# Seven-product stages of a two-block network: the way back's factors loaded through one queue into the large pool

## The chip, the cores and the metric

The kernel runs on one core of a Trainium2 chip. Its time is the device time of one execution in microseconds (us). A profile of one execution shows what each engine did: TensorE (PE, with its weight loads as PEld), VectorE (DVE), ScalarE (ACT), GpSimd (POOL) and SyncE (SP), which here only issues transfers. A transfer (DMA) is issued by an instruction in the queue of SP or ACT; if it has to wait for data or for a free buffer, that queue stands until then. TensorE's clock is throttled; the share that was granted is listed beside each stretch.

## The reference

Two network blocks over one sequence of 1024 tokens of width 1024, in float32. What matters here are the three places with a wide hidden layer:

```
h = h + square(relu(z @ w_up)) @ w_down                     # block 1: 1024 -> 4096 -> 1024
x = x + 0.5 * norm(swiglu(h, ffn1_w_in, ffn1_w_out))        # block 2: 1024 -> 2816 -> 1024
x = x + 0.5 * norm(swiglu(h, ffn2_w_in, ffn2_w_out))        # block 2: the same again
```

Between the first and the second lies a gated projection, between the second and the third a mixer with attention and a state-space model (`s5_mixer`: 32 groups of 64 complex states), whose tables depend on parameters alone.

## The kernel before

Each matrix is cut into a high and a low part (`hi` rounded on ACT, `lo` = value minus `hi` on DVE or POOL), and a product is the sum of three matmuls (hi x hi, hi x lo, lo x hi). The three wide layers use a scheme with seven products of half-size blocks instead of eight. The way up (`ups_s`, L526) writes sums of blocks of the hidden layer, the LEFT factors, to memory (`lay_by`, L607: tiles `hs`, on SP's queue). The way back, which the change touches, is `down_s` (L644). It is called three times: stage 1 for `w_down` (16 pairs of row blocks, 8 quads `q` of two), stages 2 and 3 for `ffn1_w_out` and `ffn2_w_out` (11 pairs, 6 quads, the last of one).

A stage runs its products in the order 2, 1, 5, 3, 6, 7, 4. Products 2 and 1 write four banks each, 1 in `a`; 5 and 3 accumulate in `c`; 6, 7 and 4 in `a` again. There are eight banks. When a product ends, its `out` empties banks into `Y`: a copy on ACT (L743, after products 2, 5, 3 and 4) or an addition on DVE (L744, after 1, 6, 7).

A product is a row of units, one for each quad. A unit (L702) loads a left factor `sd` from `hs` (SP, L706, into the tag `raw`, which has two buffers), obtains a right factor, cuts both into hi and lo (`pair`, L698 and L699), and gives PE 24 matmuls (L717). The right factor comes in one of two ways:

- Stage 1 (`wt`, L655, and `right`, L671): blocks of the weight `wd` are loaded on ACT's queue (L659) into the large pool `u` (32 slots of 512 KB over all partitions) and kept in `W`, so that products 5, 6, 7 and 4 form their differences in place on DVE (L673). Block 2 alone is loaded twice.
- Stages 2 and 3 (`kept`, L663): the differences were made during the way up (`rights`, L625) and lie in memory as `tw`; one load `td` for each unit, on ACT's queue (L667).

`after(ins, first)` (L299) orders the schedule alone: the program is laid out by a simulated run, in which `ins` is placed no earlier than the end of `first`; no semaphore on the chip stands for it. On the chip, each engine and queue runs its instructions in the order of the schedule and waits for data and for free slots. Loads of right factors are placed after the end of the product before the last (`ends`), or of the last product 3 of the way up (`self.late`). Left loads are placed in one chain with all other loads into `raw` (`last_raw`).

The state-space tables are made during stages 1 and 2, so that they take no time of their own: `s5_small` (L1234) and eight parts `s5_eighth` (L1337), each with a first step (a load of `xy`, which has one buffer; multiplications on DVE and POOL) and a second step (transposes L1388 and small matmuls on PE into two banks, copies on ACT, eight small transfers L1412 on SP). `aside` says ahead of which product which steps are called. A call sets the place in the program's order, which is the priority in the schedule.

Of the kernel before, what the change touches and what calls it, by code (L numbers as in the profile page):

```python
# [11 lines left out]
F32 = mybir.dt.float32  # L12
# [6 lines left out]
P = 128  # L19
# [3 lines left out]
H = 512  # L23
# [224 lines left out]
class Model:  # L248
# [395 lines left out]
    def down_s(self, hs, w, Y, done, z=None, aside={}, tail=1, tw=None):  # L644

        nc = self.nc
        v = nc.vector
        npair = w.shape[1]  # L650
        qs = [(p, min(2, npair - p)) for p in range(0, npair, 2)]
        W = {}
        ends = [self.late]

        def wt(b, q):  # L655
            if (b, q) not in W:
                p, n = qs[q]
                t = W[b, q] = self.u("wd", shape=[P, 2, H])
                d = nc.scalar.dma_start(out=t[:, :n], in_=w[b, p : p + n].rearrange("c p f -> p c f"))  # L659
                self.after(d, ends[max(len(ends) - 2, 0)])  # L660
            return W[b, q]

        def kept(p, q):  # L663
            n = qs[q][1]
            t = self.u("td", shape=[P, 2, H])
            src = tw[q][self.RIGHT[p], :n] if p in self.RIGHT else w[{2: 2, 1: 0, 3: 3}[p], 2 * q : 2 * q + n]
            d = nc.scalar.dma_start(out=t[:, :n], in_=src.rearrange("c p f -> p c f"))  # L667
            self.after(d, ends[max(len(ends) - 2, 0)])
            return t

        def right(p, q):  # L671
            n = qs[q][1]
            sub = lambda o, x, y: v.tensor_tensor(o[:, :n], x[:, :n], y[:, :n], op=ALU.subtract)  # L673
            if p == 2:
                t = wt(2, q)
                del W[2, q]
            elif p == 1:
                t = wt(0, q)
            elif p == 5:
                t = wt(0, q)  # L680
                sub(t, wt(1, q), t)
            elif p == 3:
                t = wt(3, q)
            elif p == 6:
                t = wt(0, q)
                sub(t, wt(3, q), t)
            elif p == 7:
                t = wt(1, q)
                sub(t, wt(3, q), t)
            else:  # L690
                t = wt(2, q)
                sub(t, t, wt(0, q))
            return t

        def pair(tags, x, n):
            hi, lo = (self.u("tt", F32R, [P, 2, H]) if tag == "u" else self.pw.tile([P, 2, H], F32R, name=tag, tag=tag)
                      for tag in tags)
            nc.scalar.activation(hi[:, :n], x[:, :n], AF.Copy)  # L698
            v.tensor_tensor(lo[:, :n], x[:, :n], hi.bitcast(F32)[:, :n], op=ALU.subtract)  # L699
            return hi, lo  # L700

        def unit(p, q):  # L702
            n = qs[q][1]
            g, i = self.LEFT[p]
            s = self.pr.tile([P, 2, H], F32, name="sd", tag="raw")
            d = nc.sync.dma_start(out=s[:, :n], in_=hs[q][g][i, :n].rearrange("c p f -> p c f"))  # L706
            self.after(d, self.last_raw)
            self.last_raw = d
            if tw:
                return pair(("wh", "wl"), s, n), pair(("u", "u"), kept(p, q), n)  # L710
            return pair(("wh", "wh"), s, n), pair(("wl", "wl"), right(p, q), n)

        def mm(bank, un, c, t, start, stop):
            (sh, sl), (th, tl) = un
            ts = slice(t * P, (t + 1) * P)
            for k, (x, y) in enumerate(((sh, th), (sh, tl), (sl, th))):
                self.mark = nc.tensor.matmul(bank, x[:, c, ts], y[:, c], start=start and k == 0, stop=stop and k == 2,  # L717
                                             skip_group_check=True)

        def product(p, banks, start, out, mid=None):  # L720
            nq = len(qs)
            head = nq - (tail if p == 4 else 1)
            for q in range(head):
                un = unit(p, q)
                for c in range(qs[q][1]):
                    for t in range(4):
                        mm(banks[t], un, c, t, start and q == 0 and c == 0, False)
                if q % 2 and chores:
                    chores.pop(0)()
            uns = [(q, unit(p, q)) for q in range(head, nq)]  # L730
            if mid:
                mid()
            for t in range(4):
                for q, un in uns:
                    for c in range(qs[q][1]):
                        mm(banks[t], un, c, t, start and q == 0 and c == 0, q == nq - 1 and c == qs[q][1] - 1)
                out(t)
            ends.append(self.mark)

        chores = []  # L740
        four = lambda: [self.bank() for _ in range(4)]
        A, B = slice(0, H), slice(H, D)
        copy = lambda t, sl, b: nc.scalar.activation(Y[t][:, sl], b, AF.Copy)  # L743
        plus = lambda t, sl, b: v.tensor_tensor(Y[t][:, sl], b, Y[t][:, sl], op=ALU.add)  # L744

        def also(p):
            for f in aside.get(p, ()):
                f()

        def c11(t):  # L750
            Y[t] = self.u("Y")
            copy(t, A, b[t])

        def c22(t):
            Y[4 + t] = self.u("Y")
            copy(4 + t, B, c[t])

        def c12(t):
            plus(t, B, a[t])
            chores.append(lambda: done(t))  # L760

        def c21(t):
            copy(4 + t, A, a[t])
            done(4 + t)

        also(2)
        b = four()
        product(2, b, True, c11)
        also(1)
        a = four()  # L770
        product(1, a, True, lambda t: plus(t, A, a[t]))
        also(5)
        c = four()
        product(5, c, True, c22)
        also(3)
        product(3, c, False, lambda t: copy(t, B, c[t]))
        also(6)
        product(6, a, False, c12)
        also(7)
        if z:  # L780
            chores.append(lambda: z.flush(3))
        product(7, a, False, lambda t: plus(4 + t, B, a[t]))
        also(4)
# [941 lines left out]
```

## Time and profile before

| | us |
|---|---|
| median of three runs | 3072.33 (3070.43 to 3072.9) |
| profiled execution | 3082.47 |
| its span, first to last instruction | 3080.7 |
| PE busy | 2821.6 (92%) |
| DVE, ACT, POOL busy | 1775.9, 1323.5, 868.0 |

Mean granted clock 0.963. Stage 1 lies between 603.7 and 978.0 us of the span, stage 2 between 1571.1 and 1828.8, stage 3 between 2828.4 and 3068.0. In each, the first number of a row is where it starts; "idle before <-releaser" is how long the engine had nothing to run, and which instruction or transfer ended that. A row of busy time by stretch gives its bounds and length, the busy time and the count of instructions of PE, PEld, DVE, ACT and POOL (of those asked for, where it is for one line or one tile), the granted clock, the busy share of the DMA engines and the GB/s that they moved; a row of sums gives the stretches of one stage together.

### The profile page before, as it was taken

To read this page: it belongs to the slowest core of one execution; us is meant where nothing else is said; L and a number is where in the kernel's file an instruction comes from. 1 tells how busy PE (TensorE), PEld (TensorE's weight loads), DVE (VectorE), ACT (ScalarE), POOL (GpSimd) and SP (SyncE) were. 2 spreads that over 40 slices of the span, in tenths; PEclk is the share of its full clock that TensorE was granted. 3 is DMA by queue.
4 is the path that set the end of the run, shared out by engine and by line. 5 is a ranking of instruction groups with operands and counts; after the bars stand their busy time and mean duration, and the time that the engine had idled before them with its cause. 6 is when DMAs were issued, how large, how long until landed. Compare 5 with 4: busy or idle time off the path is not lost.

```text
span 3080.7 us, 33834 instructions
## 1 busy us (share of the span) xinstructions
PE 2821.6 (92%) x12585; PEld 2306.2 (75%) x12585; DVE 1775.9 (58%) x2527; ACT 1323.5 (43%) x1921; POOL 868.0 (28%) x667
## 2 busy tenths in 40 slices
PE   8998999898999979999978999997689899998998
PEld 7777788677777858777767778886677677776776
DVE  4576655487784365665667551417635756665445
ACT  5446555433445463333324452246644533333343
POOL 3331332211222432121111031459844212211002
PEclk9999999999999989999989999998899999999999
DMA  3114344564455123454466661523113244446556
GB/s 141 61 42 137 132 146 146 201 230 144 162 183 170 55 82 103 151 177 150 146 221 212 217 220 72 168 76 110 35 48 130 86 150 158 158 157 208 181 180 209
DMA packets 192309, 443.11 MB, mean 144 GB/s; under 512 B 23220, under 2 KB 23312, under 8 KB 192144
## 3 DMA queue, kind: packets, MB, share of 16 engines
q1 hardware_dynamic: 155600, 362.83, 35.4%
q10 hardware_dynamic: 36544, 78.13, 7.2%
q8 instruction: 98, 1.61, 0.2%
q14 instruction: 67, 0.55, 0.1%
HBM read 303.92 MB, written 131.60 MB: 141 GB/s over the span
## 4 chain that ended last, share of the span: by engine, by line
PE 62%; DMA 14%; DVE 9%; ACT 6%; issue 6%; POOL 2%; SPq 1%; ACTq 0%; DVEq 0%; POOLq 0%
PE b L541 22%; PE b L717 17%; PE b L455 4%; PE b L442 4%; DMA raw<-in_f_out 3%; DMA raw<-in_f_in 3%; DMA td<-tw 2%; DMA tw<-raw 2%; PE b L1103 2%; PE b L1101 2%; PE b L1102 2%; DMA sd<-hs 1%; ACT wh L481 1%; PE b L1624 1%; DVE wl L482 1%
## 5 line engine op out<-in xcount | busy, mean ns | idle before, releaser
L541 PE MATMUL b<-zh,wh 128*128 128x512 f32 x1680 | 644.9, 397 | 30.5 <-ACT wh L481 23.1
L541 PE MATMUL b<-zh,wl 128*128 128x512 f32 x1680 | 623.3, 392 | 8.4 <-DVE wl L482 3.3
L541 PE MATMUL b<-zl,wh 128*128 128x512 f32 x1560 | 612.8, 393 | 15.4 <-DVE zl L211 15.4
L717 PE MATMUL b<-tt,wh 128*128 128x512 f32 x1232 | 392.1, 400 | 51.8 <-ACT tt L698 46.5
L541 PEld LDWEIGHTS b<-zh,wh 128*128 128x128 f32 x1680 | 319.5, 190 | 117.2 <-ACT wh L481 35.1
L541 PEld LDWEIGHTS b<-zh,wl 128*128 128x128 f32 x1680 | 316.8, 189 | 78.6 <-DVE wl L482 4.6
L717 PE MATMUL b<-wl,wh 128*128 128x512 f32 x1344 | 323.5, 402 | 40.3 <-ACT wl L698 26.3
L541 PEld LDWEIGHTS b<-zl,wh 128*128 128x128 f32 x1560 | 295.4, 189 | 79.5 <-DVE zl L211 19.2
L717 PEld LDWEIGHTS b<-wl,wh 128*128 128x128 f32 x1344 | 258.7, 194 | 102.4 <-ACT wl L698 27.8
L717 PEld LDWEIGHTS b<-tt,wh 128*128 128x128 f32 x1232 | 237.5, 194 | 106.8 <-ACT tt L698 48.9
L482 POOL TENSOR_TENSOR wl<-raw,wh 128x1024 fp32r<-128x1024 f32 x60 | 148.0, 2469 | 392.4 <-ACT wh L481 368.9
L698 ACT ACTIVATE wh<-sd 128x1024 fp32r<-128x1024 f32 x140 | 141.7, 1014 | 254.3 <-PE b L717 127.0
L717 PE MATMUL b<-tt,wl 128*128 128x512 f32 x616 | 244.1, 397 | 0.0
L352 POOL TENSOR_TENSOR wl<-raw,wh 128x1024 fp32r<-128x1024 f32 (+1 forms) x58 | 142.6, 2464 | 305.0 <-ACT wh L351 274.1
L481 ACT ACTIVATE wh<-raw 128x1024 fp32r<-128x1024 f32 x120 | 126.8, 1059 | 226.0 <-DMA raw<-in_f_in 102.6
L383 POOL TENSOR_SCALAR v<-ss 128x1 f32<-128x1 f32 x80 | 46.4, 580 | 497.6 <-ACT junk L376 493.9
L618 POOL TENSOR_TENSOR hw<-h 128x512 f32<-128x512 f32 x38 | 59.2, 1558 | 409.2 <-DVE h L1188 173.2
L699 DVE TENSOR_TENSOR tt<-td,tt 128x1024 fp32r<-128x1024 f32 x84 | 95.2, 1134 | 115.4 <-ACT tt L698 115.2
L698 ACT ACTIVATE tt<-td 128x1024 fp32r<-128x1024 f32 x84 | 83.0, 988 | 162.7 <-DMA td<-tw 86.2
L699 DVE TENSOR_TENSOR wl<-sd,wh 128x1024 fp32r<-128x1024 f32 x84 | 97.4, 1159 | 77.1 <-ACT wh L698 77.1
L505 DVE TENSOR_TENSOR s<-raw 128x512 f32<-128x512 f32 x60 | 75.2, 1253 | 115.2 <-DMA raw<-in_f_in 105.2
L717 PEld LDWEIGHTS b<-tt,wl 128*128 128x128 f32 x616 | 119.1, 193 | 25.3
(362 smaller groups left out, 5301.0 us busy)
## 6 DMA issues: line engine op xcount, KB each, us to landing
sd<-hs SPq DMA_DIRECT2D x126, 512.0 KB, 4.0
raw<-in_f_in SPq DMA_DIRECT2D x94, 512.0 KB, 3.5
raw<-in_f_out SPq DMA_DIRECT2D x44, 512.0 KB, 3.6
tw<-raw SPq DMA_DIRECT2D x44, 512.0 KB, 2.9
wd<-in_w_down ACTq DMA_DIRECT2D x40, 512.0 KB, 8.9
td<-tw ACTq DMA_DIRECT2D x40, 512.0 KB, 4.3
hs<-h SPq DMA_DIRECT2D x38, 512.0 KB, 3.3
hs<-hw SPq DMA_DIRECT2D x38, 512.0 KB, 3.1
```

The lines of the kernel that those rows point to most:

```text
L352: nc.gpsimd.tensor_tensor(l, r, h.bitcast(F32), op=ALU.subtract)
L442: nc.tensor.matmul(pp[n], w[:, k, :], z(m, k, slice(n * H, n * H + H)), start=k == 0 and w is wh and m == 0, stop=k == nk - 1 and w is wl)
L455: yield nc.tensor.matmul(pp, h[:, ts], w[:, sl], start=f == 0 and w is wh and h is hh, stop=f == len(hs) - 1 and h is hl)
L481: nc.scalar.activation(hi.rearrange("p a b -> p (a b)"), x, AF.Copy)
L482: eng.tensor_tensor(lo.rearrange("p a b -> p (a b)"), x, hi.bitcast(F32).rearrange("p a b -> p (a b)"), op=ALU.subtract)
L505: v.tensor_tensor(s1, a21, a22, op=ALU.add)
L541: self.mark = nc.tensor.matmul(bank, w, x, start=start and k == 0 and i == 0, stop=k == 3 and i == 2, skip_group_check=True)
L698: nc.scalar.activation(hi[:, :n], x[:, :n], AF.Copy)
L699: v.tensor_tensor(lo[:, :n], x[:, :n], hi.bitcast(F32)[:, :n], op=ALU.subtract)
L717: self.mark = nc.tensor.matmul(bank, x[:, c, ts], y[:, c], start=start and k == 0, stop=stop and k == 2, skip_group_check=True)
L1101: nc.tensor.matmul(pp, zh, wh[:, k % 2, :], start=k == 0, stop=False)
L1102: nc.tensor.matmul(pp, zh, wl[:, k % 2, :], start=False, stop=False)
```

## The change

All loads of the way back go through one function, `load`: on SP's queue, into the pool `u`, placed after the end of the unit that lies three (stage 1) or four (stages 2 and 3) units back; `ends` now takes one entry for each unit. The left factors leave the tag `raw` and its chain. Of the weight's blocks in stage 1 only block 0 is kept (`W[q]`); the others are loaded where they are needed, so that product 7 loads two and product 5, 6 and 4 one each. The rounded right factors of stage 1 move from the tag `wl` to the pool `u`, as in the other stages. The steps in `aside` are called after the second unit of a product instead of ahead of it.

```diff
+        ahead = 4 if tw else 3
+
+        def load(name, src, q):
             n = qs[q][1]
-            t = self.u("td", shape=[P, 2, H])
-            src = tw[q][self.RIGHT[p], :n] if p in self.RIGHT else w[{2: 2, 1: 0, 3: 3}[p], 2 * q : 2 * q + n]
-            d = nc.scalar.dma_start(out=t[:, :n], in_=src.rearrange("c p f -> p c f"))
-            self.after(d, ends[max(len(ends) - 2, 0)])
+            t = self.u(name, shape=[P, 2, H])
+            d = nc.sync.dma_start(out=t[:, :n], in_=src.rearrange("c p f -> p c f"))
+            self.after(d, ends[max(len(ends) - ahead, 0)])
             return t
 
         def right(p, q):
-            n = qs[q][1]
+            k, n = qs[q]
+            if tw and p in self.RIGHT:
+                return load("td", tw[q][self.RIGHT[p], :n], q)
+            block = lambda b: load("wd", w[b, k : k + n], q)
             sub = lambda o, x, y: v.tensor_tensor(o[:, :n], x[:, :n], y[:, :n], op=ALU.subtract)
...
+            t = block({2: 2, 1: 0, 5: 1, 3: 3, 6: 3, 7: 3, 4: 2}[p])
+            if tw or p in (2, 3):
+                return t
+            if p == 1:
+                W[q] = t
+            elif p in (5, 6):
+                sub(W[q], t, W[q])
+                return W[q]
             elif p == 7:
-                t = wt(1, q)
-                sub(t, wt(3, q), t)
+                sub(t, t, block(1))
             else:
-                t = wt(2, q)
-                sub(t, t, wt(0, q))
+                sub(t, t, W.pop(q))
             return t
...
-            s = self.pr.tile([P, 2, H], F32, name="sd", tag="raw")
-            d = nc.sync.dma_start(out=s[:, :n], in_=hs[q][g][i, :n].rearrange("c p f -> p c f"))
-            self.after(d, self.last_raw)
-            self.last_raw = d
-            if tw:
-                return pair(("wh", "wl"), s, n), pair(("u", "u"), kept(p, q), n)
-            return pair(("wh", "wh"), s, n), pair(("wl", "wl"), right(p, q), n)
+            s = load("sd", hs[q][g][i, :n], q)
+            return pair(("wh", "wl"), s, n), pair(("u", "u"), right(p, q), n)
...
                         mm(banks[t], un, c, t, start and q == 0 and c == 0, False)
+                ends.append(self.mark)
+                if q == 1:
+                    for f in aside.get(p, ()):
+                        f()
                 if q % 2 and chores:
```

The functions `wt` and `kept`, and the seven calls `also(p)` ahead of the products, are gone.

## Rows read from the trace of the kernel before

**Rows 1.** Busy time by stretch: sums over stages 1, 2, 3; two single stretches.

```profile
819.80:978.00 158.20, 147.09 (x690) 118.86 (x689) 115.54 (x197) 69.25 (x84) 40.19 (x60) 0.97 0.53 181
...
sum 374.30, PE 333.74 PEld 269.48 DVE 273.27 ACT 150.66 POOL 73.09; mean PE 47.68 PEld 38.50 DVE 39.04 ACT 21.52 POOL 10.44
...
sum 257.70, PE 227.29 PEld 185.32 DVE 151.99 ACT 112.14 POOL 43.36; mean PE 32.47 PEld 26.47 DVE 21.71 ACT 16.02 POOL 6.19
...
2977.60:3007.50 29.90, 29.90 (x134) 24.76 (x133) 14.96 (x15) 13.65 (x16) 0.00 (x0) 1.00 0.63 211
...
sum 239.60, PE 218.09 PEld 178.46 DVE 117.59 ACT 95.69 POOL 14.52; mean PE 31.16 PEld 25.49 DVE 16.80 ACT 13.67 POOL 2.07
```

**Rows 2.** PE's instructions in order of time, at the twelve longest waits.

```profile
615.15 1.22 PE L717 MATMUL b<-wl,wh 128*128 128x512 f32 x2 [11.38 <-ACT wl L698]
...
669.06 1.22 PE L717 MATMUL b<-wl,wh 128*128 128x512 f32 x2 [6.01 <-ACT wl L698]
...
769.39 1.22 PE L717 MATMUL b<-wl,wh 128*128 128x512 f32 x2 [4.86 <-ACT wl L698]
...
949.36 1.32 PE L717 MATMUL b<-wl,wh 128*128 128x512 f32 x4 [4.04 <-ACT wl L698]
...
953.05 1.22 PE L717 MATMUL b<-wl,wh 128*128 128x512 f32 x2 [2.37 <-DVE wl L699]
...
1587.56 2.95 PE L717 MATMUL b<-tt,wh 128*128 128x512 f32 x5 [16.34 <-ACT tt L698]
...
1625.50 1.59 PE L717 MATMUL b<-tt,wh 128*128 128x512 f32 x4 [3.74 <-ACT tt L698]
...
1629.45 0.80 PE L717 MATMUL b<-tt,wh 128*128 128x512 f32 x1 [2.36 <-DVE tt L699]
...
1697.25 1.22 PE L717 MATMUL b<-tt,wh 128*128 128x512 f32 x2 [5.16 <-ACT tt L698]
...
2839.62 1.65 PE L717 MATMUL b<-tt,wh 128*128 128x512 f32 x3 [11.04 <-ACT tt L698]
...
2877.28 1.22 PE L717 MATMUL b<-tt,wh 128*128 128x512 f32 x2 [5.09 <-ACT tt L698]
...
2944.86 1.65 PE L717 MATMUL b<-tt,wh 128*128 128x512 f32 x3 [5.13 <-ACT tt L698]
```

**Rows 3.** Chain that ended last, between products 2 and 1 of stage 3.

```profile
2871.55 0.04 ACT Y L743
...
2872.23 3.91 DMA td<-in_f_out
...
2876.17 1.06 ACT tt L698
```

**Rows 4.** SP's waits in stage 1: total us, times, longest.

```profile
SPq L706 <- DVE wh L699: 159.2, 37, 19.3
```

**Rows 5.** Busy time by stretch, columns as in rows 1.

```profile
2877.20:2882.20 5.00, 4.92 (x12) 3.86 (x13) 2.03 (x2) 1.08 (x2) 0.00 (x0) 0.50 0.51 161
2890.00:2895.00 5.00, 5.00 (x24) 4.14 (x23) 2.91 (x3) 2.12 (x2) 0.00 (x0) 1.00 0.51 156
...
675.00:680.00 5.00, 5.00 (x24) 4.13 (x22) 4.81 (x10) 1.06 (x1) 0.00 (x0) 1.00 1.05 388
```

**Rows 6.** Transfer issues: count, KB each, median us to landing.

```profile
sd<-hs SPq DMA_DIRECT2D x126, 512.0 KB, 4.0
```

**Rows 7.** Costliest groups in stage 1: DVE's differences of blocks.

```profile
L673 DVE TENSOR_TENSOR wd<-wd 128x1024 f32<-128x1024 f32 x32 | 37.8, 1218 | 20.3 <-DMA wd<-in_w_down 20.2
```

**Rows 8.** Transposes of the state-space parts (L1388) by stretch of stage 1.

```profile
720.70:819.80 99.10, 0.00 (x0) 0.00 (x0) 0.97 0.44 151
819.80:978.00 158.20, 2.39 (x16) 1.99 (x16) 0.97 0.53 181
```

**Rows 9.** Instructions on `s5p`, then on `s5e`, in product 5 of stage 1.

```profile
720.70:769.40 48.70, 6.36 (x28) 7.47 (x14) 1.00 0.47 155
...
720.70:769.40 48.70, 3.94 (x6) 1.00 0.47 155
```

More of the change, by code (lines that the diff above doesn't have):

```diff
@@ L653, in down_s @@
         ends = [self.late]
[L655 to L659, printed above, removed]
-                self.after(d, ends[max(len(ends) - 2, 0)])
-            return W[b, q]
-        def kept(p, q):
+        ahead = 4 if tw else 3
+        def load(name, src, q):
             n = qs[q][1]
-            t = self.u("td", shape=[P, 2, H])
-            src = tw[q][self.RIGHT[p], :n] if p in self.RIGHT else w[{2: 2, 1: 0, 3: 3}[p], 2 * q : 2 * q + n]
-            d = nc.scalar.dma_start(out=t[:, :n], in_=src.rearrange("c p f -> p c f"))
-            self.after(d, ends[max(len(ends) - 2, 0)])
+            t = self.u(name, shape=[P, 2, H])
+            d = nc.sync.dma_start(out=t[:, :n], in_=src.rearrange("c p f -> p c f"))
+            self.after(d, ends[max(len(ends) - ahead, 0)])
             return t
         def right(p, q):
-            n = qs[q][1]
+            k, n = qs[q]
+            if tw and p in self.RIGHT:
+                return load("td", tw[q][self.RIGHT[p], :n], q)
+            block = lambda b: load("wd", w[b, k : k + n], q)
             sub = lambda o, x, y: v.tensor_tensor(o[:, :n], x[:, :n], y[:, :n], op=ALU.subtract)
-            if p == 2:
-                t = wt(2, q)
[L676 to L685, printed above, removed]
-                sub(t, wt(3, q), t)
+            t = block({2: 2, 1: 0, 5: 1, 3: 3, 6: 3, 7: 3, 4: 2}[p])
[6 more added lines that the diff above has]
+                return W[q]
             elif p == 7:
-                t = wt(1, q)
-                sub(t, wt(3, q), t)
-            else:
-                t = wt(2, q)
-                sub(t, t, wt(0, q))
+                sub(t, t, block(1))
+            else:
+                sub(t, t, W.pop(q))
             return t
@@ L744, in down_s @@
         plus = lambda t, sl, b: v.tensor_tensor(Y[t][:, sl], b, Y[t][:, sl], op=ALU.add)
-        def also(p):
-            for f in aside.get(p, ()):
-                f()
         def c11(t):
@@ L764, in c21 @@
             done(4 + t)
-        also(2)
         b = four()
         product(2, b, True, c11)
-        also(1)
         a = four()
         product(1, a, True, lambda t: plus(t, A, a[t]))
-        also(5)
         c = four()
         product(5, c, True, c22)
-        also(3)
         product(3, c, False, lambda t: copy(t, B, c[t]))
-        also(6)
         product(6, a, False, c12)
-        also(7)
         if z:
@@ L782, in down_s @@
         product(7, a, False, lambda t: plus(4 + t, B, a[t]))
-        also(4)
         def rest():
```

## The prediction

> **What bounds the kernel now.** I read the busy times by stretch first, because the change touches only the three way-back stages (`down_s`). TensorE (PE) is the engine that sets the end: the reader is to see in [rows 1] that it is busy for 333.7 of 374.3 us in the first stage, 227.3 of 257.7 in the second and 218.1 of 239.6 in the third. One product of five and a half pairs without any wait took 29.90 us for its 132 matmuls (the row counts 134 with neighbours), so a matmul costs 0.227 us, a unit of 24 matmuls 5.4 us. At that rate the stages need 1344, 924 and 924 matmuls, 305 + 210 + 210 us; they take 871.6. The other 147 us are a little PE work that must stay (transposes, the state-space parts' matmuls), waits, and what follows from waits.
>
> Second I read the waits in PE's timeline [rows 2]. They are of two kinds. The stages' first matmuls wait 11.38, 16.34 and 11.04 us (38.8 together). After that, nine waits sit where a new product, or the last unit of product 4, begins: 6.01, 4.86, 4.04, 2.37 in stage 1, 3.74, 2.36, 5.16 in stage 2, 5.09, 5.13 in stage 3, together 38.8 again. Nearly all end on ACT's rounding of a RIGHT factor (`wl` or `tt`), not of a left one.
>
> Third, the chain of waits at one of them says why [rows 3]: ACT ends its copies of the finished product (`Y`, L743), which wait for PE's last matmuls; only then, at 2872.23, does it issue the load `td`, which takes 3.91 us to land, and 1.06 us later the rounded factor exists. The load is not slow; it is issued late, because it stands in ACT's queue behind evictions that need the product's end. The left loads, on SP, are held by their two buffers: SP stood 159.2 us in stage 1 at L706 until `wh` was done with one [rows 4].
>
> Last, the clock [rows 5]. Behind such a wait the granted clock is 0.50 (the 1.2 GHz level of 1.2 and 2.4): 12 matmuls in 5.00 us where a later stretch at 1.00 has 24. PE had stood idle for 5 us before it fell, and had run for about 5 us before it rose. So each wait of that kind costs 2.5 us more than its own length.
>
> **The change part by part.**
>
> *Right factors from ACT's queue to SP's, issued by units.* Removed: the issues at L659 and L667, and with them ACT's stops there. The new load may be scheduled from the end of the unit three (stage 1) or four units back, 16 us ahead at 5.4 a unit; load, rounding and subtraction need 4.0 + 2 x 1.06 + 2 x 1.2, below 9 us [rows 3, 6, 7]. That covers a product's first unit too, so the nine waits go: -38.8. They fall into seven places (4.04 with 2.37, and 3.74 with 2.36, are one place each), so 7 x 2.5 = -17.5 of half clock goes with them. Bounds: at least nothing, if the loads come no earlier; at most the 56.3 together. I take nearly all of it, because the row of the chain shows no cause beside the issue order. What is late next there is DVE's `lo` subtraction, which is not moved.
>
> *Stage starts.* The gate stays the last product 3 of the stage before, and 12 matmuls (2.7 us) of product 4 follow it. The first left load lands in 4.0, the second load behind it on the queue 512 KB later, 1.4 us at the 388 GB/s that [rows 5] shows for a burst; rounding 1.06. PE starts some 4 us after it runs out; with the stores of `hs` still in SP's queue I say 5. Gain 38.8 - 15 = -23.8. Bounds: 0, if SP stands behind those stores, to -31 with 2.7 each.
>
> The Trainium skill's page "DMA: Bandwidth & Descriptors", section "Issuing engines are not separate DMA queues", says that issuing from several engines only saves the time of issuing, usually small. On bandwidth the trace agrees: the burst above ran at a DMA share of 1.05. By that rule alone, moving loads from ACT to SP would be worth nothing, and the time would stay at 3072; the chain of waits contradicts that part, since what costs is the place in an in-order queue.
>
> *More loads.* Blocks of the first stage's right factor are kept no longer but loaded again: per four row blocks 8 loads instead of 5, over 8 quads 24 more of 512 KB. A unit asks for 1 MB in 5.4 us, 194 GB/s, in product 7 for 1.5 MB, 291 GB/s; the burst had 388. I cost them at nothing; the cover is PE's 5.4 us per unit, and where it fails a unit waits one load more, 1.4 us. For product 7 alone I add 6: one late load of 4.0 and half of its clock loss. Bounds 0 to 8 x 1.4 + 2.5 = 14.
>
> *The pool.* A unit holds four slots of `u` while it is made (two loads, two rounded halves; five in product 7) and two on PE, of 32. In product 7 of stage 1, 8 are `Y`, 8 the kept block, 4 `pT` and 4 normalised rows: 8 stay free, enough for one unit on PE, one ready and one being loaded. In the other stages no block is kept. Cost nothing; the bound is in the rivals. The left loads lose the two-buffer wait of [rows 4]; it hid behind PE already, so no gain is counted.
>
> *State-space parts inside a product.* Their PE, DVE and POOL work is the same. They need banks: products 5 and 3 hold all eight (four `a`, four `c`). Before, part 0's second step was called ahead of `c` and ran there; no transpose (L1388) runs between 720.7 and 819.8, and 16 (four parts) run after [rows 8]. Called inside product 5 it finds no bank and slides behind product 3, and part 1's first step, which needs its tile `xy`, with it. So one more first step comes into products 6, 7 and 4: on DVE 6.36 + 3.94 [rows 9] and three multiplies of some 0.66, 12.3 us. DVE was busy 115.5 of 158.2 us there [rows 1], so there is room on the mean, but each subtraction behind it comes later. Bounds 0 to +28 (12.3 and as many late subtractions again, with a clock drop). I charge 14. In stage 2 DVE was busy 152 of 258: nothing. There the part called ahead of product 2 no longer delays the start; that is in the 5 us.
>
> **Sum.** -38.8 - 17.5 - 23.8 + 6 + 14 = -60.1. The profiled execution took 3082.47 us (span 3080.7), 10.1 above the median of the three runs, 3072.33. 3082.5 - 60.1 = 3022.4, less 10.1: 3012.
>
> **The rivals.**
>
> *The starts stay.* SP carries the stores of `hs`, which wait for DVE and POOL after the last pair, and now all first loads. If these are queued behind the stores, the 23.8 is lost: 3036. For it: these stores come at once behind the last pair in the program's order; against it: the first loads are due before that pair's data exist. Chance 0.14. The Trainium skill's "Perfetto Trace Analysis", section "DMA Optimizations", advises one issuing engine for inputs and another for outputs; this change goes the other way, and by that advice this is the case to fear; no row of before shows loads and stores of these stages on one queue, beyond the left loads.
>
> *DVE becomes the bound late in stage 1.* Four first steps in products 6 and 7, ahead of the units' subtractions: 28 instead of 14, and the 8.9 of product 4's two waits with their clock stays: 3035. For it: DVE's share there is the highest of all stages. Chance 0.11.
>
> *Nothing is won.* The gates only order the schedule; no load is held or hastened by them on the chip. If loads end up as late as before, or DVE takes every wait's place, the time stays near 3072. Against it: `td` has nothing to wait for but its slot. Chance 0.07.
>
> *Slower: the pool runs dry in products 6, 7 and 4 of stage 1.* If only one unit fits beside the one on PE, load and making come one after the other: 4.0 + 1.4 + 1.2 + 1.06 + 1.2 = 8.9 us a unit against 5.4, 3.5 us for each of 24 units, 84 us: 3096. It decides the sign from 17 such units on (60 / 3.5). For it: products 6 and 7 keep 20 to 24 of 32 slots taken. Against it: 8 are enough by the count above, and stages 2 and 3 keep nothing. Chance 0.12, as the count has no margin.
>
> **How the numbers follow.** The forecast's own case has 0.56: 2985 to 3035. With 0.14 and 0.11 around 3036, 0.07 at 3072 and 0.12 above, 2985 to 3070 leaves out the slower case, a part of "nothing" and a few per cent below (if also the starts nearly vanish). A measurement tells 0.2%, 6 us, from no change: faster than 3066 has 0.56 + 0.14 + 0.11 = 0.81, within 0.07, slower 0.12.
>
> **What would show it.** Right: no load issued on ACT in these stages; PE's waits at the products' beginnings of 4 to 6 us gone and PEclk 1.00 through stage 3 after its start; first matmuls 4 to 6 us after the last of the stage before; all five parts' transposes of stage 1 after product 3. Wrong: starts still at 11 us with SP standing at L622's stores; waits of 1 to 3 us at many units of products 6, 7 and 4 that end on DVE `tt` (late part of stage 1), or on a DMA whose issue waited for a slot; SP standing at the small copies of the state-space parts with unit loads behind them.

## The result, and the profile after

The changed kernel took 3105.35 us (median of four runs, 3101.74 to 3107.08) beside 3072.61 for the kernel before on the same chip: a ratio of 1.0101 (of the means), 95% interval 1.0082 to 1.012. It is 1% slower; 3012 was forecast. The profiled execution took 3106.15 us, span 3104.3. That is 23.6 us more than the profiled execution of the kernel before, which was itself 10 us above its median; stages and tail below are of these two executions.

Busy time by stretch says where. The stretches are the products in their order; shown are products 6, 7 and 4 of stage 1, product 6 of stage 2, and each stage's sum.

```profile
797.60:880.50 82.90, 59.88 (x252) 44.85 (x249) 69.88 (x146) 22.94 (x29) 29.63 (x53) 0.84 0.62 212
880.50:947.40 66.90, 53.13 (x212) 41.33 (x212) 45.82 (x71) 23.09 (x29) 8.71 (x21) 0.87 0.63 219
947.40:998.80 51.40, 48.87 (x230) 38.77 (x231) 36.39 (x34) 25.88 (x32) 9.16 (x5) 1.00 0.53 192
sum 395.00, PE 344.79 PEld 274.10 DVE 279.65 ACT 148.84 POOL 60.63; mean PE 49.26 PEld 39.16 DVE 39.95 ACT 21.26 POOL 8.66
...
1736.10:1782.00 45.90, 36.75 (x173) 28.86 (x173) 25.49 (x55) 15.34 (x21) 6.53 (x15) 0.93 0.68 242
...
sum 249.80, PE 229.88 PEld 184.52 DVE 145.60 ACT 104.06 POOL 39.91; mean PE 32.84 PEld 26.36 DVE 20.80 ACT 14.87 POOL 5.70
...
sum 223.90, PE 217.27 PEld 176.65 DVE 105.76 ACT 88.06 POOL 7.21; mean PE 31.04 PEld 25.24 DVE 15.11 ACT 12.58 POOL 1.03
```

Product 6 of stage 2 in the kernel before:

```profile
1729.10:1760.80 31.70, 31.70 (x153) 25.99 (x153) 15.72 (x17) 15.20 (x20) 0.00 (x0) 1.00 0.68 229
```

Counted from PE's last instruction ahead of a stage to the stage's end, as the stages will be told from here on, stage 1 went from 374.6 to 397.5 us, stage 2 from 254.5 (to its last matmul at 1825.7) to 258.3, stage 3 from 239.8 to 230.2, and what follows stage 3 from 12.8 to 16.9. Products 6, 7 and 4 of stage 1 take 201.2 us where [rows 1] had 158.2 (+43), product 6 of stage 2 takes 45.9 where it had 31.7 (+14). The rest of the three stages, the waits at their starts included, is some 40 us shorter.

PE's timeline at the longest waits, against [rows 2]:

```profile
603.83 1.19 PE L700 MATMUL b<-tt,wh 128*128 128x512 f32 x4 [2.07 <-ACT tt L686]
...
812.20 0.79 PE L700 MATMUL b<-tt,wh 128*128 128x512 f32 x1 [6.60 <-DVE tt L687]
...
922.74 2.50 PE L700 MATMUL b<-tt,wh 128*128 128x512 f32 x5 [7.28 <-ACT tt L686]
...
1598.20 2.50 PE L700 MATMUL b<-tt,wh 128*128 128x512 f32 x5 [8.14 <-ACT tt L686]
...
2863.57 2.50 PE L700 MATMUL b<-tt,wh 128*128 128x512 f32 x5 [5.90 <-ACT tt L686]
...
2898.91 1.54 PE L700 MATMUL b<-tt,wh 128*128 128x512 f32 x4 [2.68 <-ACT tt L686]
```

The starts wait 2.07, 8.14 and 5.90 us instead of 11.38, 16.34 and 11.04. The waits at products' beginnings are down to between 2 and 4. New are four waits of 4.7 to 7.3 us in the middle of products 6 and 7 of stage 1, one of 5.6 in product 6 of stage 2, and one of 3.8 in product 2 of stage 1. SP's timeline around the beginning of product 6 of stage 1:

```profile
781.45 0.41 SPq L659 DMA_DIRECT2D wd<-in_w_down  x1
799.39 0.33 SPq L1370 DMA_DIRECT2D s<-s5b  x1
...
802.43 5.20 SPq L1388 DMA_DIRECT2D s5m<-kk  x8
807.67 0.58 SPq L659 DMA_DIRECT2D sd<-hs  x1
```

Between 781.9 and 807.67 no load of a unit is issued. SP stands 17.4 us at the store of part 0's `s5b`, whose transposes find no bank until product 3 ends; then come a load of `xy` and the eight small copies, and only then the next unit's `sd`. The `sd` after it, at 822.29, stands behind a load of `xy` and a store of `s5b` again. The wait of 6.60 us at 812.20 is not yet theirs: that unit's loads are the ones issued up to 781.45, and what it lacks is the low part of its right factor, which stands in DVE's order behind the tables of a part:

```profile
810.94 1.21 DVE L687 TENSOR_TENSOR tt<-wd,tt 128x1024 fp32r<-128x1024 f32 x1
```

Two groups of SP's waits in stage 1, the first answering to [rows 4]:

```profile
SPq L659 <- PE b L700: 86.3, 20, 7.0
SPq L1370 <- DVE s5b L1369: 27.7, 3, 17.4
```

Of the other groups: a load of a left factor took 4.0 us to land [rows 6], now 5.2; the differences 1218 ns on the mean [rows 7], now 1286, still 32 of them; the transposes of the parts stand in products 6, 7 and 4 again, 20 instead of 16 [rows 8]; on `s5p` in products 6 and 7 DVE has four first steps, 18.65 and 6.34 us, 112 operations (28 to a step, [rows 9]); the kernel before had three there, 85 operations:

```profile
797.60:998.80 201.20, 2.77 (x20) 2.01 (x17) 0.89 0.60 209
...
797.60:880.50 82.90, 18.65 (x84) 0.84 0.62 212
880.50:947.40 66.90, 6.34 (x28) 0.87 0.63 219
```

### The profile page after: what moved, and what is told of

Read it like the earlier page. It is cut to its first block, busy times and chain, and to the rows that moved or that the text cites. A ratio compares the mean times of both kernels' runs of the same rounds, so it can differ in the third digit from the quotient of the medians.

```text
span 3104.3 us, 33906 instructions
## 1 busy us (share of the span) xinstructions
PE 2845.8 (92%) x12585; PEld 2318.8 (75%) x12585; DVE 1784.9 (57%) x2527; ACT 1319.4 (43%) x1921; POOL 857.8 (28%) x667
## 5 line engine op out<-in xcount | busy, mean ns | idle before, releaser
L700 PE MATMUL b<-tt,wh 128*128 128x512 f32 x2128 | 694.6, 407 | 88.4 <-ACT tt L686 69.1
L700 PEld LDWEIGHTS b<-tt,wh 128*128 128x128 f32 x2128 | 414.6, 196 | 197.9 <-ACT tt L686 79.1
L700 PE MATMUL b<-tt,wl 128*128 128x512 f32 x1064 | 428.6, 403 | 0.0
L687 DVE TENSOR_TENSOR wl<-sd,wh 128x1024 fp32r<-128x1024 f32 x140 | 166.4, 1189 | 198.6 <-ACT wh L686 198.2
L700 PEld LDWEIGHTS b<-tt,wl 128*128 128x128 f32 x1064 | 209.5, 197 | 44.3
L686 ACT ACTIVATE tt<-wd 128x1024 fp32r<-128x1024 f32 x92 | 94.8, 1031 | 107.5 <-DVE wd L668 91.1
L687 DVE TENSOR_TENSOR tt<-wd,tt 128x1024 fp32r<-128x1024 f32 x92 | 112.0, 1218 | 39.7 <-ACT tt L686 39.0
L351 ACT ACTIVATE wh<-raw 128x1024 fp32r<-128x1024 f32 (+1 forms) x58 | 59.5, 1032 | 163.8 <-issue 42.6
L482 DVE TENSOR_TENSOR wl<-raw,wh 128x1024 fp32r<-128x1024 f32 x60 | 79.6, 1326 | 72.5 <-ACT wh L481 37.2
```

Source lines behind the costliest of these rows:

```text
L351: nc.scalar.activation(h, r, AF.Copy)
L482: eng.tensor_tensor(lo.rearrange("p a b -> p (a b)"), x, hi.bitcast(F32).rearrange("p a b -> p (a b)"), op=ALU.subtract)
```

## The experiments

Ratios are to the kernel before on the same chip, with 95% intervals. The runs were on several chips, on which the kernel before took 3072.6 to 3081.8 us; lengths of stages and products are of one profiled execution each. Three theories stood at first. Theory 1, banks: the parts' second steps slide to where banks are free and pile up, because of where they are called. Theory 2, queue: a unit's loads stand on SP behind state-space transfers. Theory 3, pool: products 6, 7 and 4 lack slots.

**Parts ahead of the products again, loads as after** (e1).

```diff
-                if q == 1:
-                    for f in aside.get(p, ()):
-                        f()
...
+        also(1)
         a = four()
```

> The changed kernel with the state-space steps called ahead of the products again, as before the change; the loads stay as changed. Theory 1 (banks): the parts pile up behind product 3 because inside products 5 and 3 no bank is free, and the pile costs products 6 and 7 of stage 1 some 45 us and product 6 of stage 2 some 14; called ahead of product 5, part 0 ends early again, products 6, 7 and 4 of stage 1 fall from 201 to 160 us or less, and the time is 3045 to 3068 us. Theory 2 (queue): unit loads stand behind the parts' small copies on SP wherever the parts are; the time falls by half at most, 3078 to 3095. Theory 3 (pool): too few free slots in products 6, 7 and 4, whatever the parts do; 3098 to 3108.

1.0082 (1.0062 to 1.0103). Products 6, 7 and 4 of stage 1 still take 74.0, 63.0 and 55.5 us, and product 5 takes 62.7, 46.3 in the changed kernel. In stage 2 product 6 is down to 31.9, but the start waits 16.01 us again and the stage takes 256.6. The placement alone is not the cause.

**Parts inside the products, loads as before** (e2).

```diff
-        also(1)
         a = four()
...
+                if q == 1:
+                    also(p)
                 if q % 2 and chores:
```

> The kernel before with one edit: the steps are called after the second unit of a product; all loads as before. Theory 1 (banks): the same pile behind product 3, with loads that are no better: 3095 to 3130 us. Theories 2 and 3 (queue, pool): right factors still come on ACT's queue and left ones have buffers of their own, so nothing or little is lost: 3062 to 3085.

0.9967 (0.9953 to 0.9981): this half of the change is a gain, and products 6, 7 and 4 of stage 1 take 49.4, 56.1 and 52.1. Theory 1 falls with these two; the loss comes with the loads.

**No small copies** (e3; that part of the state-space tables stays zero).

```diff
-        for r in range(8):
-            nc.sync.dma_start(out=m[16 * r : 16 * r + 16, :, 16 * (7 - r) : P], in_=kk[:, :, 0 : 16 * (r + 1)])
```

> The changed kernel without the eight small copies of each part (the blocks below the diagonal of the table are left out: the tile holds zeros). SP is rid of 64 issues of 0.6 us and of the waits for their source. Theory 2 (queue): the waits of products 6 and 7 go, 3055 to 3075 us. Theory 1 (banks): the pile on DVE and in PE's order stays, 3085 to 3104. Theory 3 (pool): 3098 to 3108.

1.0032 (1.0019 to 1.0045): 0.7% less than after, with products 6 and 7 still at 79.1 and 68.4, so the copies are a small part of it.

**Second steps only where banks are free** (e4: called by product and unit, those of stage 1 after the sixth unit of product 1, the second of 6, 7 and 4 and the sixth of 4).

```diff
-                if q == 1:
-                    for f in aside.get(p, ()):
-                        f()
+                for f in aside.get((p, q), ()):
+                    f()
```

> The changed kernel with the steps still inside products, but second steps only in products in which four banks are free: part 0's in product 1 after its sixth unit, parts 1 to 4 in products 6, 7 and 4; part 6's in product 1 of stage 2, part 7's in product 6. Theory 1 (banks): as the run with the parts ahead or better, 3040 to 3065 us. Theory 2 (queue): 3078 to 3095. Theory 3 (pool): 3098 to 3108.

1.01 (1.0076 to 1.0125). The time only moves: products 5, 6, 7 and 4 take 56.1, 63.3, 69.1 and 72.3.

**The parts' transfers off SP** (e5).

```diff
-        gate = nc.sync.dma_start(out=xy, in_=self.sxy[:, :, 64 * e : 64 * e + 64])
+        gate = nc.gpsimd.dma_start(out=xy, in_=self.sxy[:, :, 64 * e : 64 * e + 64])
```
(and the five others of `s5_eighth`)

> The kernel after, with the six kinds of transfers of a state-space part (the xy load, the stores of its tables, the eight small copies) issued by POOL instead of SP; the parts' arithmetic and the factor loads stay. Queue theory (in products 6 and 7 of stage 1 and in product 6 of stage 2 a unit's two loads stand in SP's order behind state-space transfers that wait for PE, DVE or the xy buffer, 17.4 us at one store): products 6, 7 and 4 of stage 1 come back from 82.9, 66.9 and 51.4 to about 50 each (-45 to -50), product 6 of stage 2 from 45.9 to about 33 (-13), of which some 10 us may stay for subtractions that DVE now does late: 3045 to 3060 us. DVE theory (the subtraction that makes a right factor, now done when its unit is due, stands in DVE's order behind the state-space arithmetic): only 10 to 15 us come back, 3088 to 3095 us, and the long waits of PE stay, ended by a rounding behind DVE's subtraction. Pool theory (loads come late since no buffer is free): no change, 3100 to 3110 us.

1.0026 (1.0011 to 1.004): 20 us of the span come back, 12 of them in stage 2 (product 6: 33.8), but only 4 in stage 1 (70.5, 75.7, 50.1). So SP's order was the cause in stage 2, and in stage 1 something stands behind it. SP's timeline, DVE's and PE's for one unit of product 7 in this run:

```profile
876.44 0.37 SPq L659 DMA_DIRECT2D sd<-hs  x1
878.50 0.89 SPq L659 DMA_DIRECT2D wd<-in_w_down  x2
```
```profile
890.98 0.42 DVE L1369 TENSOR_SCALAR s5b<-b 128x256 f32<-128x256 f32 x1 [3.85 <-ACT s5b L1368]
...
897.54 0.69 DVE L1332 TENSOR_TENSOR bt<-xy,s5k 128x512 f32<-128x512 f32 x1 [4.26 <-DMA s5m<-kk]
...
901.16 1.22 DVE L687 TENSOR_TENSOR wl<-sd,wh 128x1024 fp32r<-128x1024 f32 x1
...
903.50 1.22 DVE L668 TENSOR_TENSOR wd<-wd 128x1024 f32<-128x1024 f32 x1
```
```profile
905.85 2.50 PE L700 MATMUL b<-tt,wh 128*128 128x512 f32 x5 [7.82 <-ACT tt L686]
```

The loads are now issued 27 to 29 us ahead of PE. But the subtraction (L668) runs at 903.50, because DVE stood 3.85 us for a copy of the part's transposes and 4.26 us for the small copies to give a buffer back, and then made tables. PE waits 7.82 us.

**Right factors on ACT's queue, gates and pool as after** (e6).

```diff
-        def load(name, src, q):
+        def load(name, src, q, eng=nc.scalar):
...
-            s = load("sd", hs[q][g][i, :n], q)
+            s = load("sd", hs[q][g][i, :n], q, nc.sync)
```

> The kernel after, with the right factors' loads issued by ACT as in the kernel before, and the left factors' by SP; gates, pool and placement of the parts as after. Queue theory: a unit needs both halves and the left one still stands behind the state-space transfers on SP, so the waits of products 6 and 7 stay; one transfer fewer to a unit on SP is worth a few us, ACT standing at gates ahead of its roundings costs a few: 3095 to 3115 us. Rival, that one queue is too slow for both streams of factors: products 6 and 7 lose 40 us of their waits, 3060 to 3070 us. Pool theory: no change, 3100 to 3110 us.

1.0203 (1.0188 to 1.0218), slower than any theory said. The old queue without the kept blocks does not bring the old time back, so sharing one queue is not by itself the loss. ACT's longest group of waits in stage 1 is for DVE's differences:

```profile
ACT tt L686 <- DVE wd L668: 115.9, 30, 6.9
```

**Stage 1 as before, stages 2 and 3 as after, parts inside** (e8).

```diff
+            if not tw:
+                s = self.pr.tile([P, 2, H], F32, name="sd", tag="raw")
...
+                return pair(("wh", "wh"), s, n), pair(("wl", "wl"), old(p, q), n)
             s = load("sd", hs[q][g][i, :n], q)
```

> Stage 1's loads as in the kernel before (blocks kept in the pool, right ones by ACT, the left ones' two buffers, gates by products), stages 2 and 3 as after, the state-space parts inside the products as after. Queue theory: stage 1 gives what it gave with the old loads and the parts inside, 374 us, stage 2 between 250 and 258 (its product 6 still holds the part's transfers on SP), stage 3 the 230 of after, tail 17: about 3055 us (3048 to 3064). If the loads by units lose in any stage that has state-space parts, stage 2 stays above 255 and the sum is about 3062. Pool theory: stage 3 alone gains, -8 against parts inside alone, 3060 us; the theories differ here in stage 2 only.

0.9982 (0.9972 to 0.9991). Stage 1 takes 374.4 again, stage 3 229.4, stage 2 252.1 with product 6 at 41.7: the same parts in the same places cost stage 1 nothing more once its blocks are kept and loaded in the old way. The time lies above what either theory expected, though the stages came out as expected.

**Stage 1's gate six units back instead of three** (e7).

```diff
-        ahead = 4 if tw else 3
+        ahead = 4 if tw else 6
```

> The kernel after, with stage 1's gate on a unit's loads put at the end of the sixth unit before it instead of the third; nothing else. Gate theory (a lead of three units, some 22 us, is shorter than the state-space work that stands ahead of a unit's subtraction in DVE's order and of its loads in SP's): products 6 and 7 lose 20 to 30 of their 49 us, 3075 to 3085 us. Pool theory (32 buffers less 8 kept blocks and 8 output tiles leave 16, four to a unit, so no more than four units can be in flight whatever the gate says): within 5 us of 3105. If the deeper gate lets later loads take buffers that earlier ones need, slower: above 3112.

1.009 (1.0069 to 1.0111), products 6 and 7 at 83.7 and 68.7. The gate is not what makes them late; that fits theory 3 as well.

**The differences on POOL** (e10).

```diff
-            sub = lambda o, x, y: v.tensor_tensor(o[:, :n], x[:, :n], y[:, :n], op=ALU.subtract)
+            sub = lambda o, x, y: nc.gpsimd.tensor_tensor(o[:, :n], x[:, :n], y[:, :n], op=ALU.subtract)
```

> The kernel after, with the subtraction that makes a right factor in stage 1 (32 of 128x1024) moved from DVE to POOL, where one takes about twice as long; transfers stay on SP. DVE theory: the subtraction no longer stands behind state-space arithmetic and roundings in DVE's order, so the waits of PE for the rounding of a right factor in products 6, 7 and 4 of stage 1 shrink by 15 to 30 us: 3075 to 3090 us. Queue theory alone: the loads are as late as before and POOL is 1.2 us slower to a unit, no gain: 3100 to 3115 us.

1.012 (1.0103 to 1.0136), slower than either theory said. One takes 2.86 us there, and POOL stands for the loads itself (47.9 us at 16 of them), as they are still late on SP. A unit needs all its sources, and here two engines hold it instead of one; this run does not tell DVE's part.

**No parts in stage 1, all in stage 2** (e13).

```diff
-... {2: [m.s5_small], 1: step(0), 5: step(0, 1), 3: step(1, 2), 6: step(2, 3), 7: step(3, 4), 4: step(4)})
+... {2: [m.s5_small]})
...
-                 {2: step(5), 1: step(5, 6), 5: step(6, 7), 3: step(7)})
+                 {2: step(0, 0, 1), 1: step(1, 2, 2), 5: step(3, 3, 4), 3: step(4, 5), 6: step(5, 6), 7: step(6, 7), 4: step(7)})
```

> The kernel after, with all sixteen steps of the state-space parts called inside stage 2 (two or three to a product) and none in stage 1. Meeting theory (the loads by units cost nothing by themselves; they lose where state-space work meets them on SP's and DVE's orders): products 6, 7 and 4 of stage 1 fall to 45 to 50 each, stage 1 from 397 to 345 to 350, while stage 2, which now has all the parts and needs no subtraction, grows from 258 to 270 to 300: 3065 to 3095 us. Pool theory (products 6, 7 and 4 lack buffers whatever else runs): stage 1 stays above 380, and the whole above 3110.

1.0013 (1.0003 to 1.0022). Products 6, 7 and 4 of stage 1:

```profile
800.30:852.40 52.10, 47.07 (x194) 37.62 (x192) 32.24 (x28) 18.77 (x20) 5.75 (x2) 0.93 0.57 193
...
898.60:944.50 45.90, 45.85 (x210) 37.81 (x211) 35.19 (x29) 24.62 (x29) 9.17 (x5) 1.00 0.55 196
```

They take 52.1, 46.2 and 45.9, 144 us instead of 201; stage 1 340.4 instead of 397.5, with the same blocks kept in the pool and the same 24 more loads: theory 3 falls, and the traffic of the loads is not the cause either. Stage 2 grows to 293.4. In these products DVE's waits show how little room a unit made when it is due leaves:

```profile
DVE tt L687 <- ACT tt L686: 20.7, 18, 1.2
```

A unit asks DVE for a difference and two low parts, some 1.2 us each, and where DVE stands until ACT has rounded that difference, it stands 1.15 us (20.7 / 18): 4.8 of the 5.4 us that PE takes. That leaves a part's work little room beside a unit.

**Parts in stage 2, their transfers on POOL, last two units in order** (e14; e13 with e5's edit and the chain of e12).

> The run without parts in stage 1, with the parts' transfers (all in stage 2 now) issued by POOL, and the matmuls of the last two units of the kernel held to the order of the text. Queue theory for stage 2 (no subtractions there, so what holds its units is SP's order): stage 2 falls from 293 to 250 to 265, stage 1 keeps its 340, the tail falls by 4: 3045 to 3060 us. DVE theory (the arithmetic of ten more steps in DVE's order holds the roundings whatever the queue): stage 2 stays at 280 or more, 3070 us and above.

0.997 (0.9956 to 0.9984). Stage 1 341.2, stage 2 282.9, the number of the DVE theory, but not by its way: six products take 214 us, and product 4 takes 60.5 with one wait of 24.45, before which SP stood at a load of the stage's end (`xr`), with unit loads behind it:

```profile
SPq L307 <- DVE Y L1137: 53.7, 1, 53.7
```

**Tables on POOL too** (e16; e5 with the operations of `combine` moved).

```diff
-            nc.vector.tensor_tensor(f4(t), over(a), power(self.pwr, p0), op=ALU.mult)
+            nc.gpsimd.tensor_tensor(f4(t), over(a), power(self.pwr, p0), op=ALU.mult)
```

> The run with the parts' transfers on POOL, and besides the nine 128x512 operations of a part's first step (its tables) computed by POOL instead of DVE. DVE theory: with the transfers off SP's order, what is left of the loss in products 6, 7 and 4 of stage 1 (196 us against 144 without parts) is DVE's order; nine of 0.68 us less to a part, some 30 us of DVE's bursts in the stage, give back 15 to 30 us: 3060 to 3073 us. Rival: what holds DVE is not its busy time but its standing at waits of the state-space chain (a bank, a copy, a buffer), and POOL at half the speed makes these longer: no gain, 3085 to 3100 us.

1.0109 (1.0093 to 1.0125), slower than the rival said. In products 6, 7 and 4 DVE is busy for 152 us as it was in e5, though its tables are gone, since its own operations beside POOL's last longer (the left factors' low parts 1657 ns on the mean, 1218 in e5). So this run does not tell DVE's work from its standing. The longest wait of PE (28.45 us) came by a third engine: ACT stood 21 us at the square sum of a finished row, whose scratch tile is one of the five temporaries that the parts use, and the unit's rounding, at 947.35, was behind it:

```profile
941.79 1.06 ACT L376 ACTIVATE junk<-Y 128x1024 bf16<-128x1024 f32 x1 [21.01 <-DVE s5p L1356]
```
```profile
951.92 2.50 PE L700 MATMUL b<-tt,wh 128*128 128x512 f32 x5 [28.45 <-ACT tt L686]
```

**Two of DVE's waits taken away** (e17 on e5, e18 on e15 below).

```diff
-        nc.vector.tensor_scalar(out=d3[:, :, 64:128], in0=s3[:, :, 0:64], scalar1=-1.0, scalar2=None, op0=ALU.mult)
+        nc.scalar.activation(d3[:, :, 64:128], s3[:, :, 0:64], AF.Copy, scale=-1.0)
...
-        m = self.tmp("s5m", [P, 4, P])
+        m = self.u("s5m", shape=[P, 4, P])
```

> The run with the parts' transfers on POOL, and two of DVE's waits in a part taken away: the negated copy of the transposes is made by ACT beside the two others, and the tile that the small copies fill has a slot of the large pool instead of one of the five temporaries, so that the next part's tables need not wait for these copies. In that run DVE stood 8.3 and 4.3 us at these places in products 6, 7 and 4 of stage 1. Theory, DVE's standing at the parts' waits holds the units' subtractions: these 12.6 us come back, perhaps half of a lost clock with them, 3065 to 3077 us. Rival, DVE's work of a part as such holds them, standing or not: the time stays, 3082 to 3092 us.

> The fastest version so far (stage 1 as before, stages 2 and 3 by units, parts 5 to 7 on POOL, last two units in the order of the text) with the same two waits of DVE taken away. There the units' differences are formed ahead, so both theories expect little: within 4 us of 3057; if ACT's third copy or the slot taken from the kept blocks costs, 3062 to 3070.

e17: 1.0045 (1.0028 to 1.0061), the rival, 1 us above its range. The two waits are gone, and DVE stands 12.3 us for ACT's `kk` in their place; products 6, 7 and 4 take 81.3, 66.4 and 53.1. e18: 0.9967 (0.9956 to 0.9978), 0.4% above e15 and 1 us above the slower range expected.

**Two versions to beat both kernels** (e12, then e15). Both are e8 with the last two units' matmuls held to the order of the text; e12 has all parts' transfers on POOL, e15 those of stage 2 alone.

```diff
+        eng = nc.gpsimd if e > 4 else nc.sync
...
+                        last = self.mark
                         mm(banks[t], un, c, t, start and q == 0 and c == 0, q == nq - 1 and c == qs[q][1] - 1)
+                        if tail > 1 and p == 4:
+                            for i in got:
+                                self.after(i, last)
```

> Stage 1's loads as in the kernel before, stages 2 and 3 by units as after, parts inside the products, the parts' transfers issued by POOL, and the matmuls of the last two units of product 4 in stage 3 held to the order of the text, bank by bank, as the kernel before ran them. Against the run with stage 1 as before (3073): product 6 of stage 2 from 41.7 to about 33, its others with a few us less, the tail from 16.5 to about 12.5: 3055 to 3063 us. If the transfers on POOL delay the state-space arithmetic of stage 1, 374 there grows by 5 to 10 and the sum is 3065 to 3072.

> Stage 1's loads as in the kernel before with the transfers of parts 0 to 4 on SP; stages 2 and 3 by units as after with the transfers of parts 5 to 7 on POOL; the last two units of the kernel in the order of the text. The sum of the pieces measured: stage 1 374, stage 2 240 to 243, stage 3 229, tail 12.4: 3056 to 3062 us. If the pieces are not additive (POOL standing at a part's store holds something of the work behind stage 2), above 3066.

e12: 0.9965 (0.9953 to 0.9977); stage 2 240.2 and the tail 12.4 as expected, but stage 1 387.6, with one wait of 16.98 us in product 7. e15: 3057.27 us, 0.9927 (0.9912 to 0.9942), the pieces add up: stages 373.0, 238.4, 229.7, tail 13.2. It is the fastest here.

## Why the prediction was wrong

*Stage starts, -23.8:* the size came out, the way only in part. The three are 9.3, 8.2 and 5.1 us shorter, 22.6, but none waits the 5 us of the forecast (2.07, 8.14, 5.90). The runs with one half of the change tell the halves apart: with the loads alone (e1) the starts wait 5.98, 16.01 and 5.53 us, with the moved calls alone (e2) 2.70, 11.43 and 11.79. Stage 3 gained by the loads; stage 1 gains 8.7 of its 9.3 by the calls alone; stage 2 needed both (the part called ahead of its product 2 was in the forecast's 5 us). Stage 2 in e1, then in e2:

```profile
1617.09 1.22 PE L700 MATMUL b<-tt,wh 128*128 128x512 f32 x2 [16.01 <-ACT tt L686]
```
```profile
1575.24 1.65 PE L717 MATMUL b<-tt,wh 128*128 128x512 f32 x3 [11.43 <-ACT tt L698]
```

In stage 1 some of it only moved: what was called ahead now comes inside product 2, which waits 3.79 us in its middle and takes 56.6 us where it had 53.9. That the sum came so near is in part luck. The first rival did not come about here: just ahead of the first loads SP stood at a store of `hs` for 0.9 us in stage 1 and 2.0 in stage 3. With a part called ahead (stage 2 of e1) it stood there for 6.6. Stage 3 of the changed kernel:

```profile
SPq L622 <- DVE h L1164: 2.0, 1, 2.0
```

*Nine waits and half clock, -56.3:* the mechanism was right, the size not. The products other than 6, 7 and 4 of stage 1 and 6 of stage 2 became 17.5 us shorter: 10.8 in stage 1, 2.2 in stage 2, 4.5 in stage 3. Some 2.6 us stay at a boundary, since ACT rounds a new product's factors behind its copies of the old one's banks, though their loads have landed:

```profile
2894.91 2.07 ACT L730 ACTIVATE Y<-b 128x512 f32<-128x512 f32 x4 [13.62 <-PE b L700]
2896.84 1.08 ACT L686 ACTIVATE wh<-sd 128x1024 fp32r<-128x1024 f32 x1
```

The chain of [rows 3] had two links in ACT's order, the issue and the rounding; I removed one and counted both. Nor did the half clock go with the waits: in the 5 us behind this one, of 2.68, the granted clock was 0.66, with 14 matmuls instead of 24 [rows 5]. Two more waits of the kernel before, 2.56 us at 912.09 and 2.70 at 1793.61, belong in [rows 2] by their length and were not counted.

```profile
2898.90:2903.90 5.00, 4.99 (x14) 3.59 (x15) 5.00 (x6) 5.00 (x6) 0.00 (x0) 0.66 0.65 205
```

*More loads +6, state-space parts +14:* the step that failed. I priced the parts by their busy time on DVE and the loads by their bandwidth, each by itself, and wrote that there was room on the mean. By itself neither costs anything: products 6, 7 and 4 of stage 1, which had 158.2 us, take 157.6 with the moved parts and the old loads (e2), and 144.2 with the new loads and no parts (e13). Together they cost +43 there, and +14 in product 6 of stage 2.

The room was misread. Kept blocks had let DVE form all 16 differences of products 6 and 7 during product 3, in which no first step ran; in the changed kernel they are formed inside these products. DVE's differences, before (products 3, 6 and 7; the 4 in product 7 are product 4's) and after (6 and 7):

```profile
769.40:819.80 50.40, 17.32 (x16) 0.93 0.42 147
819.80:868.90 49.10, 0.00 (x0) 1.00 0.53 179
868.90:921.00 52.10, 3.89 (x4) 0.97 0.59 203
```
```profile
797.60:880.50 82.90, 9.72 (x8) 0.84 0.62 212
880.50:947.40 66.90, 9.76 (x8) 0.87 0.63 219
```

So the 115.5 us of DVE in [rows 1], from which I took the room, held none of these 16. With them, and with the one more first step that I had counted, DVE is busy for 152.1 us in products 6, 7 and 4, more than the 144.2 that they take without parts; there it is busy for 101.8.

```profile
797.60:998.80 201.20, 161.88 (x694) 124.95 (x692) 152.09 (x249) 71.91 (x87) 47.50 (x79) 0.89 0.60 209
```

It is not the pool, whose rival gave 3096 and looked nearer: without parts the same pool is fast (e13). Beyond that, units and parts meet in the orders of the same engines. That the cost needs both is shown: without parts in stage 1 the unit loads give 340 (e13), and with the same parts but kept blocks and the old loads 374 (e2, e8). SP holds a unit's loads behind transfers of the parts that wait for banks, DVE or `xy`; this is shown for stage 2 (e5, -12). In stage 1 the differences, now formed when they are due, stand in DVE's order behind the parts as well. One unit, the fifth of product 7, shows both. In the changed kernel PE waits 7.28 us for it, and DVE for its second block, issued at 915.57 just behind a store of `s5p`. In e5 its loads are issued by 890.8, but its difference runs 28 us later, in DVE's order behind a part's tables and a low part that waits for ACT; PE waits 7.79 us.

```profile
920.31 1.23 DVE L668 TENSOR_TENSOR wd<-wd 128x1024 f32<-128x1024 f32 x1 [1.77 <-DMA wd<-in_w_down]
```
```profile
918.65 1.22 DVE L668 TENSOR_TENSOR wd<-wd 128x1024 f32<-128x1024 f32 x1
```

ACT's waits for the differences, in products 6, 7 and 4, first in the changed kernel and then with the old loads (e2):

```profile
ACT tt L686 <- DVE wd L668: 63.8, 19, 6.3
```
```profile
ACT wl L698 <- DVE wd L673: 8.9, 6, 3.1
```

Not all of the 63.8 holds PE (without parts, where PE hardly waits, it is still 58.2 in 21), but the rows of e5 show one that does, 7.82 us. How the 43 divide among SP, DVE and ACT stays open. Each single relief, SP's (e5), DVE's tables (e16), two of DVE's waits (e17), gave 4 us of it, nothing, or less than nothing (e16: 222 us in these products); where the rows show why, another engine's order held the unit instead. Only taking away the meeting gave it back. Stage 1 with the old loads and without parts, and unit loads with all blocks kept (for which the pool has no room), were not tried.

Here belongs the sentence of the Trainium skill, "DMA: Bandwidth & Descriptors", "Issuing engines are not separate DMA queues", that more issuing engines only save the time of issuing. The runs differ: what the parts' transfers cost SP was standing, 17.4 us at one store, and moving them was worth 20 us of the span. The same page of the Trainium skill, "Anatomy of one DMA — SWDGE (gpsimd) path", says that a wait for a semaphore happens on the issuing sequencer before dispatch. It says so of transfers issued by POOL; SP's rows above show such a wait on SP, with a unit's loads behind it.

*The tail, not in my sum:* +4. The schedule mixed the matmuls of the last two units, so the four banks ended in two pairs instead of one by one, 2.0 us apart; held to the order of the text, the tail was 12.4 (e12).

```profile
3085.69 1.09 ACT L730 ACTIVATE Y<-b 128x512 f32<-128x512 f32 x2 [11.34 <-PE b L700]
...
3087.70 1.08 ACT L730 ACTIVATE Y<-b 128x512 f32<-128x512 f32 x2
```

## What to carry to other kernels

Before loads move to another queue, list what else is issued there, and for each transfer what it waits for: its longest wait, not its issue time, is what a load behind it can pay. Room on an engine is read from the work that will be there after the change: ask what the change moves into that stretch (here 16 differences). Work that is formed early and kept is also a reserve against the waits of other work on its engine; when it is formed only when due, count the engine's time for one unit with its standing at other engines (here 4.8 of 5.4 us) before anything is put beside it, and look at every engine that the unit passes: relief on one alone was given to the next. And split a change into its parts: here one half alone gained 0.3%, and the loads gained in stage 3, which has no parts, and in stage 2 once the parts' transfers were off SP (e15).

## What was not expected of the hardware

A multiplication of a part's tables, 128x512 on DVE with both operands in SBUF, takes 0.68 us on the median. In the changed kernel two took over four times as long, just while POOL ran two 128x1024 subtractions:

```profile
804.66 2.86 DVE L1332 TENSOR_TENSOR s5c<-xy,s5k 128x512 f32<-128x512 f32 x1
807.44 2.82 DVE L1333 TENSOR_TENSOR s5e<-xy,s5k 128x512 f32<-128x512 f32 x1
```
```profile
804.43 5.29 POOL L1006 TENSOR_TENSOR ptl<-raw,pth 128x1024 fp32r<-128x1024 f32 x2 [114.76 <-ACT pth L1005]
```

The Trainium skill's "SBUF — State Buffer", "SBUF: two separate sides", says that the two engines share a pair of ports: an operation of VectorE with two inputs in SBUF and one of GpSimd that reads SBUF lock each other out, and whichever starts first holds the pair for the whole instruction. The rows agree, 4.3 us in this place (2.86 + 2.82 - 2 x 0.68). It is part of the wait of 6.60 us at 812.20.
